# A hybrid decoder trunk: attention's TensorE work in source order, with a new pace for the work that fills it

## The chip, the core and the metric

The kernel runs on one core of a Trainium2 chip. The core has TensorE (PE; its weight loads are listed apart as PEld), VectorE (DVE), ScalarE (ACT), GpSimd (POOL) and SyncE (SP), which issues DMAs, 16 DMA engines, an on-chip memory SBUF, and a small accumulator memory PSUM of eight banks. The metric is the device time of one execution in microseconds, as the median of several runs.

## The reference

Two layers work on x (512 positions of 1024 features). With c giving shift, scale and gate vectors:

```python
h = rmsnorm(x, g_attn[layer]) * (1.0 + scale1) + shift1
o = mixer_layer(h, w_in[layer], w_out[layer], ...)
x = x + gate1 * o
h = rmsnorm(x, g_mlp[layer]) * (1.0 + scale2) + shift2
u, g = split(h @ w_up[layer])
x = x + gate2 * ((silu(causal_conv(g)) * u) @ w_down[layer])
```

The mixer projects h to queries, keys and values of 16 heads of width 64 in three groups. A (4 heads) is differential attention: two softmax maps, one subtracted from the other, with rotary embedding, and a norm of each head's output. B (6 heads) is a mixture of dilated windows, with rotary embedding. C (6 heads) has no rotary embedding but a cumulative forget bias. The heads' outputs are put side by side and multiplied with w_out. All is float32 in and out.

## The kernel before

**Numbers as pairs.** To keep float32 accuracy with a faster matmul format, a value is split into a high part (rounded, made by ACT) and a low part (the rest, made by DVE). A product is then three matmuls, hi·hi, hi·lo and lo·hi. The helper `mm3` (L250) issues them, so L251, L252 and L253 carry most of TensorE's work. Activations lie transposed, features on partitions and the 512 positions on the free axis. Weights are streamed: the class `Weights` has a plan of all chunks; SP loads a chunk of 512 KB (L148), ACT makes its high part (L174), DVE its low part (L186). `pump` is called from the matmul loops and prepares the next chunk; there are two buffers for split weights and three for raw ones.

**Attention** (`layer_attn`, L366) works on eight pairs of heads in the order B0 B1 A0 C0 A1 C1 B2 C2 (`ORDER`, L24). A pair has 8 blocks, two heads of four query blocks of 128 rows (i = 0 to 3, with 128(i+1) key columns). For a block b:

- `emit_S`: the scores, two matmuls into a PSUM bank of `ps_s` (two banks). An A pair has two maps, each with a bank of its own.
- `emit_max` (DVE L641) adds the mask and takes the row maximum; `emit_exp` (ACT L654) makes the exponential and its sum; for A, `emit_norm` (DVE L667 to L669) combines the maps.
- `emit_T`: i+1 transposes on TensorE (L682); `emit_hi` (ACT L701) and `emit_lo` (DVE L706) split the result into pth and ptl, for odd i two blocks at once.
- `emit_PV`: the products with V (L728, L729), for odd i only, into the one bank of `ps_o`.
- `head_post` (L733): two steps move a head's result out of PSUM (ACT L736, DVE L741); after the pair's second head the denominators are turned (transposes, L754), multiplied in (L756), an A pair is normalised (L763 on), and the result is split into the pair o[idx] (L240, L242).

**The loop** (L806 to L843) runs over the 64 blocks and two more. Pass b emits the transposes of block b-2, the maximum and exponential of block b, the scores of block b+1, and the P·V of block b-2. In three places it calls `fill`, which gives TensorE work of another kind. For pair idx that is: the Q and the K projection of the next pair (`qk_chunk`, 8 steps of three 512-column matmuls each), and for the first six pairs half a V projection (`v_half`, 4 steps of twelve 256-column matmuls), and in the eighth pair the output projection over the first seven pairs' results (`out_part`, 7 steps, the seventh of which needs o[6]). `fill` adds a share of the pair's cost to a credit; while the credit is over 0.3 it takes a step and subtracts 0.65 (1.3 for a V step). The shares are 0.06, 0.055 and 0.055, so 0.17 a block. Each step, and each call without one, also calls `tick`, which lets every post-processing generator in `aux` emit one step more.

**Post-processing of a projection** (`qk_post`, L446): for A and B, ACT copies the bank (L456), two DMAs swap neighbouring partitions (L458, L459), and three DVE operations apply the rotary embedding (L462 to L466). Then for B `stack_gen` splits the heads (L423, L420, L434, L436); for A the split (L240, L242) is spread by twelve DMAs of 64 KB a side (L477). For C `stack_gen` reads the bank itself, and two small DMAs add the bias rows (L443). `ready` emits what is left of this before a pair's first score.

**PSUM.** The three `mm` banks serve the projections, V's two accumulators and the first three output chunks. V's two are held from an even pair's fill to the end of the next pair's.

**What sets the order.** The source only gives an order of emission. A scheduler at build time decides each engine's order from its estimate of when things are ready, with earlier-emitted work first; on the chip each engine then runs its list in that order. `tc.issue_after(ins)` binds what is emitted inside it to stand behind `ins` on the same engine.

Of the kernel before, what the change touches and what calls it, by code (L numbers as in the profile page):

```python
# [30 lines left out]
def kernel(  # L31
# [53 lines left out]
    def tick():  # L85
        for g in list(aux):
            if next(g, StopIteration) is StopIteration:
                aux.remove(g)
# [6 lines left out]
    ident = cst[:, C_ID:C_ID + 128]  # L95
# [20 lines left out]
    for l in range(DEPTH):  # L116
# [9 lines left out]
        nout = 5  # L126
# [118 lines left out]
    def pair_tiles(pool, tag, name):  # L245
        hi = pool.tile([128, SEQ], F32R, tag=tag, name=name + "h")
        lo = pool.tile([128, SEQ], F32R, tag=tag, name=name + "l")
        return hi, lo

    def mm3(ps, w, rhs, first, last, c=slice(0, SEQ)):  # L250
        T.matmul(ps[:, c], w[0], rhs[0][:, c], start=first, stop=False, skip_group_check=True)  # L251
        T.matmul(ps[:, c], w[0], rhs[1][:, c], start=False, stop=False, skip_group_check=True)  # L252
        T.matmul(ps[:, c], w[1], rhs[0][:, c], start=False, stop=last, skip_group_check=True)  # L253

    def feat_q(ps, w, act, first=True, last=True, k0=0):
        n = len(act)
# [109 lines left out]
    def layer_attn(l, ap, mods, st, rt0):  # L366
# [21 lines left out]
        def v_half(q, half):  # L388
            nb, n = (1, VZ) if q == 0 else (2, 256)
            if half == 0:  # L390
                pools = {"m": (mm, "mm"), "t": (ps_t, "pt"), "o": (ps_o, "o")}
                vps[q] = [pools[c][0].tile([128, SEQ], F32, tag=pools[c][1], name="vps")
                          for c in ("otmt" if q == 0 else "mm")]
            pss = vps[q]
            w = W.use()
            for j in range(4):
                k = 4 * half + j
                wc = w(n * j, n * j + n)
                for tb in range(4):
                    b = slice(128 * tb, 128 * tb + 128)  # L400
                    d = pss[tb // nb][:, 256 * (tb % nb):256 * (tb % nb) + n]
                    go = k == 0 and tb % nb == 0
                    en = k == KC - 1
                    T.matmul(d, h[k][0][:, b], wc[0], start=go, stop=False, skip_group_check=True)
                    T.matmul(d, h[k][0][:, b], wc[1], start=False, stop=False, skip_group_check=True)
                    T.matmul(d, h[k][1][:, b], wc[0], start=False, stop=en, skip_group_check=True)
                W.pump(j)
                yield
            if half == 1:
                if q == 0:  # L410
                    for tb in range(4):
                        V.tensor_tensor(out=z[:, tb, :], in0=pss[tb][:, 256:VZ], in1=fb[:, l, :], op=ALU.add)
                vvs[q] = ap.tile([128, 4, 4, 128], F32R, tag="vv", name="vv", bufs=2)
                aux.append(v_post(q, lambda tb: pss[tb // nb][:, 256 * (tb % nb):256 * (tb % nb) + 256]))
# [153 lines left out]
        def out_part(m):  # L568
            ops[m] = mm.tile([128, SEQ], F32, tag="mm", name="ops") if m < 3 else ps_s.tile([128, SEQ], F32, tag="s", name="ops")
            w = W.use()  # L570
            for k in range(7):
                while o[k] is None:
                    tick()
                mm3(ops[m], w(128 * k, 128 * k + 128), o[k], k == 0, False)
                W.pump(k)
                yield

        fills = []
        for idx in range(8):
            f = []  # L580
            if idx < 7:
                f += [qk_chunk(idx + 1, 0), qk_chunk(idx + 1, 1)]
            if idx < 6:
                f += [v_half(idx // 2 + 1, idx % 2)]
            if idx == 7:
                f += [out_part(m) for m in range(nout)]
            cost = (10.4 if idx < 7 else 9.08) + (5.2 if idx < 6 else 0)
            fills.append([f, cost, 0.0])

        def fill(idx, share):  # L590
# [20 lines left out]
        def emit_S(b):  # L611
            idx, kind, hh, i = blocks[b]
            q, k = qks[idx, 0], qks[idx, 1]
            n = 128 * (i + 1)
            qb = slice(128 * i, 128 * i + 128)
            if kind != "A":
                s = ps_s.tile([128, SEQ], F32, tag="s", name="s")
                T.matmul(s[:, 0:n], q[hh][:, qb], k[hh][:, 0:n], start=True, stop=False)
                if kind == "B":
                    T.matmul(s[:, 0:n], q[hh][:, qb], k[2 + hh][:, 0:n], start=False, stop=True)  # L620
                else:
                    T.matmul(s[:, 0:n], q[2 + hh][0:68, qb], k[2 + hh][0:68, 0:n], start=False, stop=True)
                S[b] = [s]
                return
            res = []
            for mp in range(2):
                s = ps_s.tile([128, SEQ], F32, tag="s", name="s")
                T.matmul(s[:, 0:n], q[2 * hh + mp][0:96, qb], k[2 * hh + mp][0:96, 0:n], start=True, stop=True)  # L628
                res.append(s)
            S[b] = res  # L630

# [41 lines left out]
        def emit_T(b):  # L673
            i = blocks[b][3]
            e = E.pop(b)
            if i == 1:
                pt = pts[b - 1][0]
            else:
                pt = ps_t.tile([128, SEQ], F32, tag="pt", name="pt")
            for j in range(i + 1):  # L680
                c = 128 * (i + j) if i < 2 else 128 * j
                T.transpose(pt[:, c:c + 128], e[:, 128 * j:128 * j + 128], ident)  # L682
            if i % 2 == 0:
                n = (384, 1024)[i // 2]
                pts["cur"] = tuple(ap.tile([128, n], F32R, tag="%s%d" % (t, i), name=t, bufs=1) for t in ("pth", "ptl"))
            pts[b] = (pt,) + pts["cur"]
# [21 lines left out]
        def emit_PV(b):  # L708
            idx, kind, hh, i = blocks[b]
            if i % 2 == 0:  # L710
                return
            half = i // 2
            _, pth, ptl = pts.pop(b)
            pts.pop(b - 1)
            if half == 0:
                po_t["cur"] = ps_o.tile([128, SEQ], F32, tag="o", name="po")
            po = po_t["cur"]
            while running("v_post"):
                tick()
            vv = vvs[idx // 2]  # L720
            hd = 2 * (idx % 2) + hh
            nj = 2 * half + 2
            for j in range(nj):
                c0 = 128 if j == nj - 1 else 0
                oc = slice(256 * half + c0, 256 * half + 256)
                a = 256 * j if half == 0 else 256 * j + c0
                pc = slice(a, a + 256 - c0)
                T.matmul(po[:, oc], vv[:, j, hd, :], pth[:, pc], start=(j == 0), stop=False, skip_group_check=True)  # L728
                T.matmul(po[:, oc], vv[:, j, hd, :], ptl[:, pc], start=False, stop=(j == nj - 1), skip_group_check=True)  # L729
            if half == 1:  # L730
                aux.append(head_post(idx, kind, hh, po))

# [69 lines left out]

        emit_S(0)
        lag = 2
        f1, f2, f3 = 0.06, 0.055, 0.055
        for b in range(nb + lag):  # L806
            idx = blocks[min(b, nb - 1)][0]
            while idx and fills[idx - 1][0]:
                fill(idx - 1, 1.0)
            p = b - lag  # L810
            if l == 0 and b == 6:
                lpt.append(mrp.tile([128, 1024], F32, tag="raw", name="lp")[:, 0:256].rearrange(
                    "p (l j d) -> p l j d", l=DEPTH, j=4))
                nc.sync.dma_start(out=lpt[0], in_=lamp)
            if l == 0 and b == 10:
                with tc.issue_after(anchor[0]), tc.issue_after(anchor[1]):
                    prep()
            if b == 3:
                aux.append(after(fz_post()))
            if p >= 0:  # L820
                emit_T(p)
            if b < nb:
                emit_max(b)
            if p >= 0:
                emit_hi(p)
            fill(idx, f1)
            if b < nb:
                emit_exp(b)
            if p >= 0:
                emit_lo(p)  # L830
            fill(idx, f2)
            if b + 1 < nb:
                ready(b + 1)
                emit_S(b + 1)
            if b < nb:
                emit_norm(b)
            fill(idx, f3)
            if p >= 0:
                emit_PV(p)
            ms, mr = 4, 1.75  # L840
            if b >= ms:
                for _ in range(int((b - ms + 1) * mr) - int((b - ms) * mr)):
                    next(modg, None)  # L843
        aux.append(modg)
        for idx in range(8):
            while fills[idx][0]:
                fill(idx, 1.0)
        while any(g.__name__ == "head_post" for g in aux):
# [332 lines left out]
```

## Time and profile before

| | |
|---|---|
| median of 3 runs | 1338.02 us (1337.93 to 1339.64) |
| profiled execution | 1334.63 us, its span 1332.9 us |
| granted TensorE clock, mean | 0.989 |
| PE, PEld busy | 1277.8 us, 1058.6 us |
| DVE, ACT busy | 858.2 us, 642.3 us |
| attention loop, layer 0 and layer 1 | about 60 to 285 us, 700 to 922 us |

A row of the timeline has start, length, engine, line, operation, what it writes and reads, and how many were merged; in brackets stands how long the engine was idle before it and what ended that. A row by windows has the stretch, its length, the busy time of each engine with its number of instructions, the share of the TensorE clock that was granted, the busy share of the DMA engines and their rate. Matmuls are pipelined and their ends are modelled: the distance between two starts says more than the length of one.

### The profile page before, as it was taken

To read this page: it belongs to the slowest core of one execution; us is meant where nothing else is said; L and a number is where in the kernel's file an instruction comes from. 1 tells how busy PE (TensorE), PEld (TensorE's weight loads), DVE (VectorE), ACT (ScalarE), POOL (GpSimd) and SP (SyncE) were. 2 spreads that over 40 slices of the span, in tenths; PEclk is the share of its full clock that TensorE was granted. 3 is DMA by queue.
4 is the path that set the end of the run, shared out by engine and by line. 5 is a ranking of instruction groups with operands and counts; after the bars stand their busy time and mean duration, and the time that the engine had idled before them with its cause. 6 is when DMAs were issued, how large, how long until landed. Compare 5 with 4: busy or idle time off the path is not lost.

```text
span 1332.9 us, 17722 instructions
## 1 busy us (share of the span) xinstructions
PE 1277.8 (96%) x6568; PEld 1058.6 (79%) x6568; DVE 858.2 (64%) x1600; ACT 642.3 (48%) x1158; POOL 22.9 (2%) x16
## 2 busy tenths in 40 slices
PE   4899999999999999999999999999999999999997
PEld 1788888788877778888898888878878888888886
DVE  6888999868888874423347788875754444443232
ACT  5576677745333243322336677785543333333231
POOL 5100000000000000000000000000000000000000
PEclk8899999999999999999999999999999999999999
DMA  9345454433888853332432334212133333332331
GB/s 373 140 141 183 152 180 136 130 110 129 269 261 266 267 173 95 91 103 87 117 110 95 90 103 141 66 56 90 48 109 96 97 95 95 95 91 87 103 99 63
DMA packets 56601, 174.39 MB, mean 131 GB/s; under 512 B 8130, under 2 KB 10450, under 8 KB 56516
## 3 DMA queue, kind: packets, MB, share of 16 engines
q1 hardware_dynamic: 55364, 172.16, 41.0%
q8 instruction: 52, 0.85, 0.3%
q10 hardware_dynamic: 1088, 1.05, 0.2%
q14 instruction: 33, 0.27, 0.1%
q0 software_dynamic: 64, 0.06, 0.0%
HBM read 159.41 MB, written 2.10 MB: 121 GB/s over the span
## 4 chain that ended last, share of the span: by engine, by line
PE 53%; DMA 8%; DVE 7%; ACT 4%; issue 3%; SPq 0%; DVEq 0%; ACTq 0%
DMA rawm<-in_wmod_dram 7%; PE dps L251 6%; PE dps L253 6%; PE dps L252 6%; PE pu L251 4%; PE pu L253 4%; PE pu L252 4%; PE pg L252 4%; PE pg L253 4%; PE pg L251 4%; DVE wlo L186 1%; DVE rawm L217 1%; PE qkps L251 1%; PE qkps L252 1%; PE qkps L253 1%
## 5 line engine op out<-in xcount | busy, mean ns | idle before, releaser
L186 DVE TENSOR_TENSOR wlo<-raww,whi 128x1024 fp32r<-128x1024 f32 (+3 forms) x188 | 224.2, 1193 | 241.0 <-ACT whi L174 236.5
L174 ACT ACTIVATE whi<-raww 128x1024 fp32r<-128x1024 f32 (+3 forms) x188 | 194.5, 1035 | 329.6 <-PE dps L252 137.7
L253 PE MATMUL pu<-hh,wlo 128*128 128x512 f32 (+1 forms) x368 | 141.2, 384 | 3.5 <-DVE wlo L186 3.5
L252 PE MATMUL pg<-hl,whi 128*128 128x512 f32 (+1 forms) x368 | 143.0, 389 | 1.5 <-DVE hl L300 1.5
L251 PE MATMUL pg<-hh,whi 128*128 128x512 f32 (+1 forms) x368 | 141.6, 385 | 1.6 <-ACT whi L174 1.6
L251 PE MATMUL pu<-hh,whi 128*128 128x512 f32 (+1 forms) x368 | 142.4, 387 | 0.5 <-ACT whi L174 0.5
L253 PE MATMUL pg<-hh,wlo 128*128 128x512 f32 (+1 forms) x368 | 140.9, 383 | 1.1 <-DVE wlo L186 1.1
L252 PE MATMUL pu<-hl,whi 128*128 128x512 f32 (+1 forms) x368 | 140.7, 382 | 0.0
L251 PE MATMUL dps<-mh,whi 128*128 128x512 f32 x308 | 121.5, 395 | 0.0
L253 PE MATMUL dps<-mh,wlo 128*128 128x512 f32 x308 | 121.5, 394 | 0.0
L252 PE MATMUL dps<-ml,whi 128*128 128x512 f32 x308 | 121.2, 393 | 0.0
L217 DVE CUSTOM_DVE_ANT_0 rawm<-rawm,scb,bm 128x1024 f32<-128x1024 f32 x80 | 102.3, 1279 | 23.7 <-DMA rawm<-in_wmod_dram 23.4
L654 ACT ACTIVATE e<-e,nm 128x256 f32<-128x256 f32 (+3 forms) x160 | 89.0, 557 | 33.0 <-DVE nm L641 29.9
L251 PE MATMUL qkps<-hh,whi 128*128 128x512 f32 x224 | 95.1, 424 | 4.7 <-ACT qk L434 4.1
L898 ACT ACTIVATE y<-y 128x512 f32<-128x512 f32 x44 | 27.8, 632 | 142.6 <-DVE y L895 142.6
L252 PE MATMUL qkps<-hl,whi 128*128 128x512 f32 x224 | 89.7, 400 | 0.0
L253 PE MATMUL qkps<-hh,wlo 128*128 128x512 f32 x224 | 89.6, 400 | 0.0
L253 PEld LDWEIGHTS pu<-hh,wlo 128*128 128x128 f32 x368 | 69.1, 188 | 22.1 <-DVE wlo L186 6.9
L641 DVE CUSTOM_DVE_ANT_0 e<-s,cst 128x256 f32<-128x256 f32 (+3 forms) x160 | 76.4, 481 | 12.0 <-PE s L628 3.7
L252 PEld LDWEIGHTS pg<-hl,whi 128*128 128x128 f32 x368 | 69.0, 188 | 17.7 <-DVE hl L300 3.1
L253 PEld LDWEIGHTS pg<-hh,wlo 128*128 128x128 f32 x368 | 69.0, 188 | 16.7 <-DVE wlo L186 1.9
L251 PEld LDWEIGHTS pg<-hh,whi 128*128 128x128 f32 x368 | 69.1, 188 | 16.0 <-ACT whi L174 2.0
(176 smaller groups left out, 2663.2 us busy)
## 6 DMA issues: line engine op xcount, KB each, us to landing
raww<-in_wup_dram SPq DMA_DIRECT2D x88, 512.0 KB
rawm<-in_wmod_dram SPq DMA_DIRECT2D x80, 512.0 KB
raww<-in_wqk_dram SPq DMA_DIRECT2D x32, 512.0 KB
raww<-in_wdown_dram SPq DMA_DIRECT2D x32, 512.0 KB
mu<-in_wmod_dram SPq DMA_DIRECT2D x16, 512.0 KB
raww<-in_wout_dram SPq DMA_DIRECT2D x16, 448.0 KB
raww<-in_wv_dram SPq DMA_DIRECT2D x12, 512.0 KB
raww<-in_wdown_dram SPq DMA_DIRECT2D x16, 384.0 KB
```

What stands on the lines that cost most here:

```text
L174: A.activation(out=h[:, 0:m], in_=self.raw[i][:, c:c + m], func=AF.Copy)
L186: V.tensor_tensor(out=lo[:, 0:m], in0=raw[:, c:c + m], in1=h[:, 0:m].bitcast(F32), op=ALU.subtract)
L217: V.tensor_tensor_reduce(out=raw, in0=raw, in1=scb, scale=1.0, scalar=bm[:, l, ci:ci + 1], op0=ALU.mult, op1=ALU.add, accum_out=dst)
L251: T.matmul(ps[:, c], w[0], rhs[0][:, c], start=first, stop=False, skip_group_check=True)
L252: T.matmul(ps[:, c], w[0], rhs[1][:, c], start=False, stop=False, skip_group_check=True)
L253: T.matmul(ps[:, c], w[1], rhs[0][:, c], start=False, stop=last, skip_group_check=True)
L641: anchor[0] = V.tensor_tensor_reduce(out=e[:, 0:n], in0=s[:, 0:n], in1=cst[:, mask + SEQ - n:mask + SEQ], scale=-scale, scalar=3e38, op0=A ...
L654: anchor[1] = A.activation(out=e[:, 0:n], in_=e[:, 0:n], func=AF.Exp, bias=nm, scale=-1.0, accum_out=den).ins
L898: last_silu[0] = A.activation(out=y, in_=y, func=AF.Silu).ins
```

## The change

Five things change, all in `mm3` and `layer_attn`.

1. TensorE's matmuls and transposes in the loop are issued through a helper that binds each to stand behind the one before it, while `row[0]` is set (during the block loop). The matmuls in `head_post` and `fz_post` are not.
2. P·V of a block is emitted a pass later, at the end of pass b for block b-3; the loop has one pass more.
3. The fill shares depend on the block within the pair. They sum to 1 over the eight blocks, where they summed to 1.36; the first four blocks get 0.61, or 0.68 when the next pair is an A pair. The costs change accordingly.
4. Six of the seven steps of the first output chunk move from the eighth pair to the seventh. In the eighth come six steps of the second chunk, then the seventh step of the first, the seventh of the second, and the third chunk. Chunks four and five come after the loop.
5. Each pass begins with four more ticks.

```diff
+    row = [False, None]
+
+    def pe(ins):
+        with (tc.issue_after(row[1]) if row[0] and row[1] else ExitStack()):
+            r = ins()
+        row[1] = r.ins
+
+    def mmul(*a, **k):
+        pe(lambda: T.matmul(*a, **k))
+
     def mm3(ps, w, rhs, first, last, c=slice(0, SEQ)):
-        T.matmul(ps[:, c], w[0], rhs[0][:, c], start=first, stop=False, skip_group_check=True)
...
+        mmul(ps[:, c], w[0], rhs[0][:, c], start=first, stop=False, skip_group_check=True)
...
+        def part(g, n):
+            for _ in range(n):
+                next(g)
+                yield
+
+        outs = [out_part(m) for m in range(nout)]
+        near = [0.155, 0.155, 0.15, 0.15, 0.12, 0.1, 0.085, 0.085]
+        far = [0.18, 0.18, 0.17, 0.15, 0.09, 0.08, 0.075, 0.075]
+        share = [far if idx < 7 and ORDER[idx + 1][0] == "A" else [0.125] * 8 if idx == 7 else near for idx in range(8)]
...
+            if idx == 6:
+                f += [part(outs[0], 6)]
             if idx == 7:
-                f += [out_part(m) for m in range(nout)]
-            cost = (10.4 if idx < 7 else 9.08) + (5.2 if idx < 6 else 0)
+                f += [part(outs[1], 6)] + outs[0:3]
+            cost = (10.4, 9.75)[idx // 7] + (5.2 if idx < 6 else 3.9 if idx == 6 else 0)
...
-        f1, f2, f3 = 0.06, 0.055, 0.055
-        for b in range(nb + lag):
+        row[0] = True
+        for b in range(nb + lag + 1):
             idx = blocks[min(b, nb - 1)][0]
+            f1 = f2 = f3 = share[idx][b % 8] / 3 if b < nb else 0.0
+            for _ in range(4):
+                tick()
...
-            if p >= 0:
-                emit_PV(p)
+            if p >= 1:
+                emit_PV(p - 1)
...
+        row[0] = False
         aux.append(modg)
         for idx in range(8):
+            if idx == 7:
+                fills[idx][0] += outs[3:]
             while fills[idx][0]:
```

The other matmuls of the loop (V, scores, P·V) and the transposes are wrapped in the same way.

More of the change, by code (lines that the diff above doesn't have):

```diff
@@ L248, in pair_tiles @@
         return hi, lo
+    row = [False, None]
[5 more added lines that the diff above has]
+        pe(lambda: T.matmul(*a, **k))
     def mm3(ps, w, rhs, first, last, c=slice(0, SEQ)):
-        T.matmul(ps[:, c], w[0], rhs[0][:, c], start=first, stop=False, skip_group_check=True)
-        T.matmul(ps[:, c], w[0], rhs[1][:, c], start=False, stop=False, skip_group_check=True)
-        T.matmul(ps[:, c], w[1], rhs[0][:, c], start=False, stop=last, skip_group_check=True)
+        mmul(ps[:, c], w[0], rhs[0][:, c], start=first, stop=False, skip_group_check=True)
+        mmul(ps[:, c], w[0], rhs[1][:, c], start=False, stop=False, skip_group_check=True)
+        mmul(ps[:, c], w[1], rhs[0][:, c], start=False, stop=last, skip_group_check=True)
     def feat_q(ps, w, act, first=True, last=True, k0=0):
@@ L403, in v_half @@
                     en = k == KC - 1
-                    T.matmul(d, h[k][0][:, b], wc[0], start=go, stop=False, skip_group_check=True)
-                    T.matmul(d, h[k][0][:, b], wc[1], start=False, stop=False, skip_group_check=True)
-                    T.matmul(d, h[k][1][:, b], wc[0], start=False, stop=en, skip_group_check=True)
+                    mmul(d, h[k][0][:, b], wc[0], start=go, stop=False, skip_group_check=True)
+                    mmul(d, h[k][0][:, b], wc[1], start=False, stop=False, skip_group_check=True)
+                    mmul(d, h[k][1][:, b], wc[0], start=False, stop=en, skip_group_check=True)
                 W.pump(j)
@@ L617, in emit_S @@
                 s = ps_s.tile([128, SEQ], F32, tag="s", name="s")
-                T.matmul(s[:, 0:n], q[hh][:, qb], k[hh][:, 0:n], start=True, stop=False)
+                mmul(s[:, 0:n], q[hh][:, qb], k[hh][:, 0:n], start=True, stop=False)
                 if kind == "B":
-                    T.matmul(s[:, 0:n], q[hh][:, qb], k[2 + hh][:, 0:n], start=False, stop=True)
+                    mmul(s[:, 0:n], q[hh][:, qb], k[2 + hh][:, 0:n], start=False, stop=True)
                 else:
-                    T.matmul(s[:, 0:n], q[2 + hh][0:68, qb], k[2 + hh][0:68, 0:n], start=False, stop=True)
+                    mmul(s[:, 0:n], q[2 + hh][0:68, qb], k[2 + hh][0:68, 0:n], start=False, stop=True)
                 S[b] = [s]
@@ L627, in emit_S @@
                 s = ps_s.tile([128, SEQ], F32, tag="s", name="s")
-                T.matmul(s[:, 0:n], q[2 * hh + mp][0:96, qb], k[2 * hh + mp][0:96, 0:n], start=True, stop=True)
+                mmul(s[:, 0:n], q[2 * hh + mp][0:96, qb], k[2 * hh + mp][0:96, 0:n], start=True, stop=True)
                 res.append(s)
@@ L681, in emit_T @@
                 c = 128 * (i + j) if i < 2 else 128 * j
-                T.transpose(pt[:, c:c + 128], e[:, 128 * j:128 * j + 128], ident)
+                pe(lambda: T.transpose(pt[:, c:c + 128], e[:, 128 * j:128 * j + 128], ident))
             if i % 2 == 0:
@@ L727, in emit_PV @@
                 pc = slice(a, a + 256 - c0)
-                T.matmul(po[:, oc], vv[:, j, hd, :], pth[:, pc], start=(j == 0), stop=False, skip_group_check=True)
-                T.matmul(po[:, oc], vv[:, j, hd, :], ptl[:, pc], start=False, stop=(j == nj - 1), skip_group_check=True)
+                mmul(po[:, oc], vv[:, j, hd, :], pth[:, pc], start=(j == 0), stop=False, skip_group_check=True)
+                mmul(po[:, oc], vv[:, j, hd, :], ptl[:, pc], start=False, stop=(j == nj - 1), skip_group_check=True)
             if half == 1:
@@ L819, in layer_attn @@
                 aux.append(after(fz_post()))
-            if p >= 0:
+            if 0 <= p < nb:
                 emit_T(p)
@@ L823, in layer_attn @@
                 emit_max(b)
-            if p >= 0:
+            if 0 <= p < nb:
                 emit_hi(p)
@@ L828, in layer_attn @@
                 emit_exp(b)
-            if p >= 0:
+            if 0 <= p < nb:
                 emit_lo(p)
@@ L837, in layer_attn @@
             fill(idx, f3)
-            if p >= 0:
-                emit_PV(p)
+            if p >= 1:
+                emit_PV(p - 1)
             ms, mr = 4, 1.75
```

## The prediction, made before the changed kernel was run

> **What bounds the kernel now.** I read the page first, then busy time by stage, then the timeline of one engine at a time around the places where TensorE stands still.
>
> ```profile
> span 1332.9 us, 17722 instructions
> PE 1277.8 (96%) x6568; PEld 1058.6 (79%) x6568; DVE 858.2 (64%) x1600; ACT 642.3 (48%) x1158; POOL 22.9 (2%) x16
> ```
>
> TensorE bounds the whole, but 96% hides where it is loose, because pipelined matmuls are drawn longer than their spacing. The stages, two attention loops and a stretch of MLP; the columns are stretch, length, busy time of PE, PEld, DVE, ACT, POOL, clock, DMA share and rate:
>
> ```profile
> 60.00:285.00 225.00, 217.19 (x1299) 184.53 (x1298) 199.85 (x482) 161.28 (x355) 0.00 (x0) 0.99 0.50 157
> 700.00:922.00 222.00, 217.62 (x1339) 185.53 (x1338) 174.58 (x434) 159.79 (x356) 0.00 (x0) 1.00 0.30 90
> 980.00:1280.00 300.00, 300.00 (x1299) 243.65 (x1299) 126.80 (x146) 103.86 (x131) 0.00 (x0) 1.00 0.32 95
> 114.00:222.00 108.00, 103.14 (x619) 87.67 (x618) 102.27 (x257) 78.74 (x180) 0.00 (x0) 0.98 0.55 169
> 142.10:146.10 4.00, 3.96 (x14) 3.40 (x15) 3.43 (x11) 1.20 (x3) 0.00 (x0) 0.57 0.69 217
> ```
>
> The MLP stretch has 1299 matmuls in 300 us and no hole: 0.231 us each, nothing to win. The change touches only the two attention loops, 447 us together. There VectorE is the second engine: 102.3 of 108 us busy in the middle of layer 0.
>
> What a matmul really costs is the distance between starts:
>
> ```profile
> 244.01 0.39 PE L252 MATMUL qkps<-hl,whi 128*128 128x512 f32 x1
> 244.24 0.39 PE L253 MATMUL qkps<-hh,wlo 128*128 128x512 f32 x1
> 138.34 0.28 PE L404 MATMUL vps<-whi,hh 128*128 128x256 f32 x1
> 138.46 0.28 PE L405 MATMUL vps<-wlo,hh 128*128 128x256 f32 x1
> 259.26 0.66 PE L754 MATMUL pr<-cst,dx 128*128 128x128 f32 x4
> 259.67 0.31 PE L622 MATMUL s<-qk 68*128 68x128 f32 x1
> ```
>
> So 0.23 us for 512 columns, 0.12 for 256 (0.45 ns a column), and 0.41 for four transposes, 0.10 each. A head pair, from the loops of the code: 48 projection matmuls 11.0, 48 V matmuls 5.8, scores over 5120 columns 2.3, 20 transposes 2.05, P·V (16 of 256 columns, 8 of 128) 2.4, the pair's four denominator transposes 0.41. Sum 24.0 us; 18.2 for the seventh pair, which has no V. How long the pairs took is read from the first score matmul of the first and of the eighth pair, in layer 0 and in layer 1:
>
> ```profile
> 64.62 0.22 PE L618 MATMUL s<-qk 128*128 128x128 f32 x1
> 250.79 0.45 PE L618 MATMUL s<-qk 128*128 128x128 f32 x2
> 716.22 0.33 PE L618 MATMUL s<-qk 128*128 128x128 f32 x1
> 894.82 0.33 PE L618 MATMUL s<-qk 128*128 128x128 f32 x1 [0.27 <-ACT qk L434]
> ```
>
> Seven pairs took 186.2 and 178.6 us, for 6 x 24.0 + 18.2 = 162.2 of work: 24.0 and 16.4 lost, 40.4 together. That is what an order can win at most in this stretch. I estimate 8 of it as common to both kernels: the forget gate's small matmuls, the subnorm ones, and work pulled across the ends.
>
> **Where the time goes between pairs.** The next pair's scores need its K projection, which is post-processed on ACT, VectorE and SP. For the third pair (an A pair), from its last projection matmul to its first score:
>
> ```profile
> 105.74 0.40 PE L253 MATMUL qkps<-hh,wlo 128*128 128x512 f32 x1
> 108.32 0.59 ACT L456 ACTIVATE qf<-qkps 128x512 f32<-128x512 f32 x1
> 112.03 0.69 DVE L462 TENSOR_TENSOR qf<-qf,rope 128x512 f32<-128x512 f32 x1 [0.24 <-DMA sw<-qf]
> 115.41 0.62 ACT L240 ACTIVATE sw<-qf 128x512 fp32r<-128x512 f32 x1
> 116.06 0.69 DVE L242 TENSOR_TENSOR qf<-qf,sw 128x512 fp32r<-128x512 f32 x1 [0.78 <-ACT sw L240]
> 117.35 1.85 SPq L477 DMA_DIRECT2D qk<-sw  x3
> 122.89 0.29 PE L628 MATMUL s<-qk 96*128 96x128 f32 x1
> ```
>
> From 105.97 (the end of the last projection) to 122.89 is 16.9 us. TensorE did not stand still: the scheduler had pulled the pair after next's Q projection ahead of this score. The same chain in layer 1, and that of a B pair at its longest and shortest:
>
> ```profile
> 754.97 0.39 PE L253 MATMUL qkps<-hh,wlo 128*128 128x512 f32 x1
> 769.45 0.23 PE L628 MATMUL s<-qk 96*128 96x128 f32 x1
> 76.77 0.40 PE L253 MATMUL qkps<-hh,wlo 128*128 128x512 f32 x1
> 90.93 0.22 PE L618 MATMUL s<-qk 128*128 128x128 f32 x1
> 216.47 0.39 PE L253 MATMUL qkps<-hh,wlo 128*128 128x512 f32 x1
> 227.44 0.33 PE L618 MATMUL s<-qk 128*128 128x128 f32 x1
> ```
>
> 14.3 for A; 13.9 and 10.7 for B.
>
> **The change, part by part.** No matmul, transpose, load or copy is added or removed. What moves:
>
> *Order (row, pe, mmul).* Inside the loop each wrapped TensorE instruction must follow the one before it in the source, so the pulling ahead ends. If data is late, everything behind waits. The transposes of head_post and the forget gate's matmuls are not wrapped and still float.
>
> *Pace (share) and four more ticks a block.* I followed the fill rule by hand: a step is taken while the credit is over 0.3 and costs 0.65 (1.3 for V). The credit was 0.17 of the pair's cost a block, is now 0.155, 0.155, 0.15, 0.15 (0.18, 0.18, 0.17, 0.15 ahead of an A pair). The sixteen projection steps still end at the edge of the fourth and fifth block, but V's four steps spread over blocks four to seven, counted from zero, instead of ending in the fifth. From a pair's first score to the end of its last projection lie then 11.0 of projection, 1.1 of transposes, 1.2 of scores, 1.2 of P·V and 0.4 of denominators: 14.9 us (15.2 where the last step falls a block later). Behind it V and the rest make 9 us of cover, and then comes the next pair's first score, in fixed order. A pair lasts the larger of 24.0 and 14.9 plus the chain.
>
> How long the chain will be the trace does not say; bounds. Upper: as measured. Lower for A, adding the rows' own steps without queueing: copy 0.6; copy start to the first product 112.03 - 108.32 - 0.59 = 3.1 for the swap through DMA; three products of 0.69, 2.1; split 0.6 and 0.7; and 117.35 to 122.89, 5.5, for the transfers of the split halves: 12.6. For B, without those transfers and with four half-tile steps of about 0.65 (as the split rows): 8.4, so 15.2 + 8.4 lies under 24.0. I take the low ends: seven ticks a block instead of three issue a pair's Q post-processing and its SP transfers up to two blocks sooner (they ended only just ahead of K's on SP), and VectorE, whose queue stretched the rest, gets its turn whenever TensorE waits. C pairs have no swap, and I give them no loss. Four A boundaries (two a layer): 14.9 + 12.6 - 24.0 = 3.5 each, 14.0.
>
> *The bank wait.* This stop goes, as the first projection of the pair may no longer be pulled ahead of the bank's last reader:
>
> ```profile
> 139.73 0.30 PE L682 MATMUL pt<-cst,e 128*128 128x128 f32 x1
> 142.14 0.66 PE L251 MATMUL qkps<-hh,whi 128*128 128x512 f32 x1 [2.11 <-ACT qk L434]
> ```
>
> It is part of the 40.4 above and not counted again.
>
> *Q to K in odd pairs.* There V's two accumulators hold two of the three mm banks, so K's first matmul needs Q's bank copied out first. In the new pace Q's last and K's first step fall into one fill call, with nothing between. Now:
>
> ```profile
> 97.41 0.39 PE L253 MATMUL qkps<-hh,wlo 128*128 128x512 f32 x1
> 97.61 1.06 ACT L174 ACTIVATE whi<-raww 128x1024 fp32r<-128x1024 f32 x1 [1.08 <-PE qkps L252]
> 98.58 0.58 ACT L456 ACTIVATE qf<-qkps 128x512 f32<-128x512 f32 x1
> 99.21 0.50 PE L251 MATMUL qkps<-hh,whi 128*128 128x512 f32 x1
> ```
>
> 1.57 us from 97.64 to 99.21, mostly covered by P·V. Bare it costs 0.6 (the copy) to 1.57 (a weight split ahead of it). I take 0.75, nearer the copy: emitted first. Six times: 4.5.
>
> *V products a block later.* A late lo of the last transposed block no longer holds TensorE; its gain is part of the 40.4. I leave 2 us of waits of this kind.
>
> *Output projection from the seventh pair on.* Six of its steps cover the seventh pair's empty blocks (in the 40.4 again). wout's loads are issued in the same sequence, only earlier; SP carries them ahead of nothing that waits, POOL has none. But by the fill rule the seventh step, which needs the seventh pair's output, falls one block after that pair's last P·V. The chain now:
>
> ```profile
> 257.61 0.28 PE L729 MATMUL po<-ptl,vv 128*128 128x128 f32 x1
> 261.36 0.50 PE L251 MATMUL ops<-oh,whi 128*128 128x512 f32 x1 [0.23 <-ACT oh L240]
> ```
>
> 3.75 us, and in fixed order only two transposes (0.2) and the denominators (0.4) fill it: 3.1, of which 0.3 is paid now. The third output chunk's weights wait for the first's buffer: another 0.5. Two layers: 6.6. It could be nothing, if floating transposes and spare ticks bring the output sooner.
>
> A stop has a second price: after the 2.11 us above the granted clock was 0.57 for 4 us (the row 142.10:146.10), 1.7 us lost. The Trainium skill (TensorE: Matmul & The Clock Gate, "The HAM clock gate") says a whole idle window of about 3.4 us halves the clock. The 0.57 came after a shorter stop, so the trace shows less idling suffices; by the rule the 3.1 us waits would escape, by the row two of them would lose 3.4 us more, an estimate outside the sum.
>
> **Sum.** New losses in the pairs: common 8.0 + A boundaries 14.0 + Q to K 4.5 + rest 2.0 = 28.5 against 40.4: 11.9 gained. Outside: 6.6 lost. Net -5.3. The profiled execution took 1334.63 us (its span 1332.9), 3.4 under the median of 1338.02; it would come to 1329.3, and the median to **1332.7**. A measurement of this kernel tells about 0.2%, 2.7 us.
>
> **The rivals.** *Slower: the chain stays as long as measured, and TensorE may not go around it.* Place: the first score of every A and B pair. A: (16.9 + 14.3)/2 = 15.6, so 14.9 + 15.6 - 24.0 = 6.5, four times 26.0; B: (13.9 + 10.7)/2 = 12.3, so 15.2 + 12.3 - 24.0 = 3.5, four times 14.0. That is 26.0 above the low ends: 1359. It decides from a chain 0.7 us (5.3 over eight boundaries) above the low ends; B has 0.4 us of slack more. For it: VectorE at 95% in layer 0. Against: ticks and layer 1's idler VectorE. 0.32.
>
> *VectorE sets layer 0's pace.* In 114 to 222 it had 5.7 us to spare, so layer 0 gains little however TensorE is ordered: half of the 11.9 goes, 1338.7, no change. With the cases in between: 0.16.
>
> *More is won:* no wait for the output, no bare copies, chains shorter than the rows: 5.3 + 6.6 + 4.5, 1322 or better. 0.14.
>
> *The order changes nothing, because the scheduler already kept it:* the trace speaks against that; a projection started at 142.14 ahead of waiting work of the pair before. 0.02, within no change. My forecast: 0.36.
>
> **Numbers.** Faster 0.36 + 0.14 = 0.50, same 0.18, slower 0.32. The range takes in the better case with some of its A boundaries gone (1316) and most of the slower one (1355); the forecast's own is 1326 to 1337.
>
> **What would show it.** Right: score matmuls of A pairs waiting 2 to 5 us for SP's transfers, twice a layer; a 3 us wait of the output projection for oh in the eighth pair; short waits for qf; the L434 bank stop gone; seven pairs in about 180 and 173 us; an MLP stretch unchanged. Wrong: projections still ahead of scores; boundary waits of 6 us, or none; lost time elsewhere than at these places.

## The result: 7% slower

The changed kernel took 1428.98 us (median, 1425.79 to 1431.32), the kernel before 1338.53 in the same comparison: ratio 1.0677, 95% interval 1.0660 to 1.0695. The forecast had another sign, and 1428.98 lies outside its range. First the page of the profile after, and three stretches by windows (both loops and MLP; the columns are those of the prediction):

```profile
span 1427.0 us, 17757 instructions
PE 1298.2 (91%) x6568; PEld 1081.0 (76%) x6568; DVE 868.3 (61%) x1600; ACT 641.8 (45%) x1158; POOL 22.9 (2%) x16
```

```profile
60.00:330.00 270.00, 223.99 (x1287) 193.02 (x1286) 202.75 (x480) 159.60 (x353) 0.00 (x0) 0.92 0.42 129
760.00:1010.00 250.00, 209.56 (x1202) 180.12 (x1203) 166.74 (x411) 151.32 (x341) 0.00 (x0) 0.92 0.25 74
1080.00:1400.00 320.00, 320.00 (x1386) 259.81 (x1385) 133.98 (x155) 110.51 (x142) 0.00 (x0) 1.00 0.31 94
```

MLP is what it was (320 us for 1386 matmuls, 0.231 each). The windows of the loops hold somewhat fewer matmuls in more time than those of the prediction, with PE busy 83 and 84% and a granted clock of 0.92 where it was 0.99 and 1.00. The first scores of the first and eighth pair, layer 0 and layer 1:

```profile
64.48 0.27 PE L258 MATMUL s<-qk 128*128 128x128 f32 x1
297.43 0.34 PE L258 MATMUL s<-qk 128*128 128x128 f32 x2
762.95 0.33 PE L258 MATMUL s<-qk 128*128 128x128 f32 x1 [3.37 <-ACT qk L444]
985.95 0.34 PE L258 MATMUL s<-qk 128*128 128x128 f32 x2
```

Seven pairs took 233.0 and 223.0 us, where it was 186.2 and 178.6: 91.2 us more, of the 94.1 between the two profiled spans. What TensorE stood waiting for, as us in total, number of times and longest (the rows of the loops from 2.9 us on):

```profile
PE s L258 <- DMA qk<-qf: 38.1, 8, 9.5
PE pf L547 <- DVE z L539: 9.4, 2, 5.4
PE qkps L258 <- ACT qf L466: 8.4, 6, 1.4
PE pr L775 <- ACT dx L770: 8.1, 9, 1.6
PE s L258 <- ACT qk L446: 5.8, 4, 2.3
PE s L258 <- ACT qk L444: 4.2, 2, 3.4
PE sbps L784 <- ACT osq L781: 4.0, 3, 1.5
PE s L258 <- DVE nm L662: 3.4, 4, 1.4
PE ops L258 <- ACT oh L240: 2.9, 2, 1.4
```

The first row is the four first scores of the A pairs (each of two maps). The second pair's end shows how it comes about. TensorE, ACT and DVE first, then SP's queue (L468 is K's swap, L487 are the transfers of the split halves; those from 119.82 on are Q's):

```profile
120.51 0.39 PE L258 MATMUL qkps<-hh,wlo 128*128 128x512 f32 x1
122.57 0.59 ACT L466 ACTIVATE qf<-qkps 128x512 f32<-128x512 f32 x1
129.76 0.28 PE L258 MATMUL vps<-whi,hl 128*128 128x256 f32 x1
133.26 0.68 DVE L472 TENSOR_TENSOR qf<-qf,rope 128x512 f32<-128x512 f32 x1
139.49 0.47 PE L258 MATMUL s<-qk 96*128 96x128 f32 x1 [9.46 <-DMA qk<-qf]
142.75 0.45 PE L258 MATMUL s<-qk 96*128 96x128 f32 x1 [2.79 <-DMA qk<-qf]
```

```profile
119.82 1.24 SPq L487 DMA_DIRECT2D qk<-sw  x2
...
126.80 0.59 SPq L487 DMA_DIRECT2D qk<-sw  x1
127.48 0.54 SPq L468 DMA_DIRECT2D sw<-qf  x1
...
136.17 1.20 SPq L487 DMA_DIRECT2D qk<-sw  x2
```

K's last projection ends at 120.74. Its copy is done at 123.16, but SP is issuing Q's twelve transfers, about 0.6 us each, until 127.4; only then comes K's swap. From projection to score are 18.7 us, and the work written into the order ends at 130: TensorE stands 9.46 us, then 2.79 for the second map.

### The profile page after: what moved, and what is told of

It reads as the page before. It is cut to its first block, busy times and chain, and to the rows that moved or that the text cites. A ratio compares the mean times of both kernels' runs of the same rounds, so it can differ in the third digit from the quotient of the medians.

```text
span 1427.0 us, 17757 instructions
## 1 busy us (share of the span) xinstructions
PE 1298.2 (91%) x6568; PEld 1081.0 (76%) x6568; DVE 868.3 (61%) x1600; ACT 641.8 (45%) x1158; POOL 22.9 (2%) x16
## 4 chain that ended last, share of the span: by engine, by line
PE 52%; DMA 7%; DVE 7%; ACT 4%; issue 3%; SPq 0%; DVEq 0%; ACTq 0%
PE dps L258 16%; PE pu L258 12%; PE pg L258 12%; DMA rawm<-in_wmod_dram 6%; PE qkps L258 4%; PE ops L258 3%; PE vps L258 2%; DVE wlo L186 2%; DVE rawm L217 1%; PE s L258 1%; ACT whi L174 1%; PE pt L703 1%; ACT e L675 1%; PE po L258 1%; DMA raww<-in_wvz_dram 1%
## 5 line engine op out<-in xcount | busy, mean ns | idle before, releaser
L258 PE MATMUL s<-qk 128*128 128x128 f32 (+11 forms) x256 | 68.1, 338 | 51.9 <-DMA qk<-qf 38.1
L258 PE MATMUL qkps<-hh,whi 128*128 128x512 f32 x224 | 98.8, 441 | 8.4 <-ACT qf L466 8.4
L258 PEld LDWEIGHTS s<-qk 128*128 128x128 f32 (+2 forms) x256 | 47.6, 198 | 63.1 <-issue 19.4
L258 PE MATMUL qkps<-hh,wlo 128*128 128x512 f32 x224 | 90.7, 405 | 0.0
```

What stands on the lines that cost most here:

```text
L258: pe(lambda: T.matmul(*a, **k))
```

## Experiments

Each run's ratio is against the kernel before, run beside it (1335.8 to 1337.0 us in the five comparisons). "After" is the changed kernel.

**Order alone.** Pace, ticks, P·V and the output projection as before.

```diff
-            f1 = f2 = f3 = share[idx][b % 8] / 3 if b < nb else 0.0
-            for _ in range(4):
-                tick()
+            f1, f2, f3 = 0.06, 0.055, 0.055
...
-            if p >= 1:
-                emit_PV(p - 1)
+            if p >= 0:
+                emit_PV(p)
```

> The kernel before with nothing but the fixed TensorE order: old pace (0.17 a block), three ticks a block, P.V in the pass of its transposes, output projection in the eighth pair. Theory 1 (in a fixed order TensorE must stand at each pair's first score until that pair's Q and K are post-processed, and standing halves its clock): the stops at the first scores stay (48 us in the changed kernel), stops at P.V and in V's empty blocks come on top, 1410 to 1470 us. Theory 2 (the new pace, the extra ticks and the moved pieces disturb ACT, VectorE and SP, and the order itself is harmless): 1335 to 1360 us.

1424.41 us, ratio 1.0658 (1.0611 to 1.0705). The order by itself costs nearly all that the change costs, as the first theory said. Here P·V, still in its old place, held TensorE too; in the kernel after, P·V has one row of waits, 1.3 us for DVE's step out of its bank, and with the old ticks or the old pace in that order it is 0.7 and 0.6 us.

```profile
PE po L258 <- DVE ptl L725: 8.8, 12, 1.3
PE po L258 <- ACT pth L720: 5.5, 2, 3.0
```

**No order, all the rest.**

```diff
-        row[0] = True
```

> The changed kernel with only the fixed order taken out again; pace, ticks, later P.V and moved output projection stay. Theory 1: the loss goes nearly all, 1325 to 1350 us. Theory 2: most of it stays, 1390 us or more.

1359.66, ratio 1.0167 (1.0132 to 1.0202), between the two expectations. The rest is not free either; that it adds so little to the order means that it also gives something back there, P·V's waits among it.

**No order, no extra ticks.**

```diff
-        row[0] = True
...
-            for _ in range(4):
-                tick()
```

> The changed kernel without the fixed order and without the four extra ticks a block: new pace, later P.V and moved output projection are left, and the scheduler orders TensorE as before. With the order free and the ticks in, the time was 1359.7, 24 us above the kernel before. If the ticks make those 24 us (they issue post-processing in bunches), it comes to 1330-1342. If pace or later P.V make them, it stays at 1352-1364.

1341.12, ratio 1.0031 (1.0021 to 1.0042): the ticks make 18 of the 22 us.

**Only later P·V and the moved output projection.** The edit above and the old pace:

```diff
+            if idx < 7:
+                f1, f2, f3 = 0.06, 0.055, 0.055
```

> The changed kernel without the fixed order, without the extra ticks and with the old pace in the first seven pairs: later P.V and the moved output projection are all that is left. With the new pace in, the time was 1341.1, 4.5 us above the kernel before. If the new pace is what is left of the loss there, this gives 1328-1337; if the later P.V is, 1340-1346; if the new pace won something under a free order, 1346-1360.

1336.23, ratio 0.9994 (0.9980 to 1.0009): these two parts are worth nothing measurable, and the new pace costs 0.4% where the order is free.

**Projections out of the order.** The matmuls of `feat_q` and `v_half` go out as `T.matmul`, unbound; the attention's own stay bound. One line of several:

```diff
-                    mmul(d, h[k][0][:, b], wc[0], start=go, stop=False, skip_group_check=True)
+                    T.matmul(d, h[k][0][:, b], wc[0], start=go, stop=False, skip_group_check=True)
...
```

> The changed kernel, with the projection matmuls (Q, K and V of the pairs to come) out of the fixed list: they are tied to nothing and nothing is tied to them; scores, transposes, P.V and the output projection stay in their written order among themselves. Extra ticks and pace stay. Theory of the lost cover (what the scheduler used to move into the stops were projection matmuls): most of what the order costs beyond the free version's 1359.7 goes, 1355-1380. Rival (the order among the attention's own matmuls holds the score back, and floating projections can't help since the scheduler sees another time than the chip): 1400-1430.

1378.55, ratio 1.0321 (1.0286 to 1.0356). 50 us of the order's price is the binding of the projections, as the theory of the lost cover says; binding the attention's own matmuls makes the other 19. The cover can be seen: 11.1 us of projections run without a break up to the first A pair's first score, where the kernel after stood 9.46 us.

```profile
118.15 0.39 PE L261 MATMUL qkps<-hh,whi 128*128 128x512 f32 x1
...
129.00 0.40 PE L263 MATMUL qkps<-hh,wlo 128*128 128x512 f32 x1
129.47 0.22 PE L258 MATMUL s<-qk 96*128 96x128 f32 x1
```

Its waits have no row for scores waiting for DMA at all, while the bank stop at a head split, gone in after, is back:

```profile
PE s L258 <- DVE nm L662: 10.8, 12, 1.7
...
PE qkps L261 <- ACT qk L444: 4.4, 2, 2.3
```

**Order without the extra ticks.**

```diff
-            for _ in range(4):
-                tick()
```

> The changed kernel without the four extra ticks a block. Theory 1: the stops at the first scores stay or grow (post-processing is issued later), the two stops at the forget gate's matmuls (9.4 us) go: 1410 to 1450 us. Theory 2, if the ticks are what disturbs: under 1380 us.

1391.26, ratio 1.0410 (1.0365 to 1.0455): both theories missed; in the fixed order the ticks cost 38 us. Two rows of its waits against after's 38.1 and 9.4:

```profile
PE s L258 <- DMA qk<-qf: 9.6, 6, 3.5
PE pf L547 <- DVE z L539: 2.6, 2, 1.7
```

On SP K's swap now goes out behind Q's first three transfers:

```profile
116.21 0.51 SPq L487 DMA_DIRECT2D qk<-qf  x1
116.89 0.51 SPq L468 DMA_DIRECT2D sw<-qf  x1
```

From K's last projection to an A pair's first score it is 12.6, 12.8, 13.2 and 12.6 us here, and yet 54 us stay.

**Q's transfers on GpSimd's queue,** in four kernels: after, after without the order, after without the ticks, and before.

```diff
-                        nc.sync.dma_start(out=res[m][32 * j:32 * j + 32, :].bitcast(F32), in_=t[r, :].bitcast(F32))
+                        (G if side == 0 else nc.sync).dma_start(out=res[m][32 * j:32 * j + 32, :].bitcast(F32), in_=t[r, :].bitcast(F32))
```

> The changed kernel, with the twelve transfers that stack the Q side of an A pair issued by GpSimd instead of SyncE. Theory of the queue (the extra ticks put Q's twelve transfers on SP's queue ahead of K's two swap transfers, 127.48 instead of about 122.6 in the second boundary, and the score's stop of 9.5 us follows from that): K's swap goes out about 5 us sooner at the four A boundaries, the waits s<-DMA qk<-qf fall from 38.1 us to about 20, and with the clock that goes with it the time falls by 20 to 30 us, to 1399-1409. Theory of the order alone (the score has its place in the list and the chain behind K's copy is long in any case, VectorE and ScalarE being busy with other steps): K-end to score stays at 18 to 21 us and the time within 6 us of 1429.

> The changed kernel without the fixed order, ticks kept (1359.7), with Q's twelve transfers issued by GpSimd. The ticks cost 18.6 us there, and the A pairs' K-end to score is 18.9 to 22.7 us with them against 15.8 to 16.8 without. If the ticks cost by putting Q's transfers ahead of K's swap on SP, most of that comes back: 1342-1349. If they cost in another way (bunched steps on VectorE and ScalarE), 1354-1362.

> The changed kernel without the extra ticks (fixed order kept, 1391.3), with Q's twelve transfers issued by GpSimd. With the ticks the same edit gained 16 us. If SP's queue is blocked only because of the ticks, nothing is left to gain: 1387-1395. If the serial issue of the twelve transfers holds K's swap in any case, 8 to 16 us: 1375-1383.

> The kernel before, with the twelve transfers that stack the Q side of an A pair issued by GpSimd instead of SyncE; nothing of the change. There K's swap transfers stood behind only two of Q's twelve in the second boundary (about 1.2 us). If SP's queue is a price in any case, about 2 to 4 us at each of four A boundaries come back: 1322-1331. If it costs only together with the extra ticks, no difference: 1333-1340. If GpSimd issues later than SP or its transfers take longer, so that Q's stacks become the last to land: above 1340.

| kernel | plain, us | Q on GpSimd, us | ratio to before |
|---|---|---|---|
| after | 1428.98 | 1412.58 | 1.0560 (1.0544 to 1.0575) |
| after, no order | 1359.66 | 1346.53 | 1.0083 (1.0054 to 1.0111) |
| after, no ticks | 1391.26 | 1394.40 | 1.0439 (1.0409 to 1.0468) |
| before | 1336.69 | 1336.16 | 0.9998 (0.9985 to 1.0012) |

The edit gains 16 and 13 us with the extra ticks and nothing without them. So SP's queue costs through the ticks: they issue Q's transfers in one block, ahead of K's swap. In the free order the row of K's first swap, with Q on SP and with Q on GpSimd:

```profile
118.70 0.54 SPq L468 DMA_DIRECT2D sw<-qf  x1
```

```profile
112.42 0.47 SPq L468 DMA_DIRECT2D sw<-qf  x1
```

6.3 us sooner, 1.7 of them because the pair itself began sooner (its first score at 93.74 instead of 95.46). In the fixed order it is less than half of the ticks' 38 us, and 16 is under the 20 to 30 expected. The four chains fall to 16.4, 13.5, 16.0 and 13.3 us, two of them still well above those without the ticks: at the second pair's end K's swap goes out at 120.83, but the first split transfer only at 131.06, 10.2 us later, where it was 8.7 in the kernel after.

**The forget gates' matmuls.** With seven ticks a block they come to TensorE before their operand (after, first layer):

```profile
83.86 0.27 PE L258 MATMUL po<-ptl,vv 128*128 128x128 f32 x1
89.53 0.56 PE L547 MATMUL pf<-z,cst 128*128 128x6 f32 x2 [5.40 <-DVE z L539]
```

```diff
-            for _ in range(4):
+            for _ in range(12):
                 yield
             pf = ps_t.tile([128, SEQ], F32, tag="pt", name="pf")
```

> The changed kernel with eight more empty steps (12 instead of 4) between the forget gates' last vector operation and their matmuls in the first pair of each layer. With seven ticks a block the sixteen small matmuls come to TensorE 5.40 and 4.01 us before their operand is there, then run at half clock (84.1 to 93.8 us in the first layer, 9.7 us against 4.2 without the ticks). If that is a price of its own, 10 to 16 us come back: 1413-1419. If the score behind them would have waited anyway for the K chain, which runs on ScalarE and VectorE meanwhile, 0 to 5: 1424-1430.

1423.77, ratio 1.0650 (1.0613 to 1.0687), the second theory by its number. But the edit hardly did what it should, since these matmuls are unbound and the scheduler placed them early again (their stops fell only from 9.4 to 6.8 us, both layers together):

```profile
89.77 0.36 PE L547 MATMUL pf<-z,cst 128*128 128x6 f32 x2 [4.10 <-DVE z L539]
```

What this stop costs in full stays open.

**First score unbound.** The matmuls of a pair's first score block go out unbound.

```diff
+            mm_ = T.matmul if hh == 0 and i == 0 else mmul
...
-                mmul(s[:, 0:n], q[2 * hh + mp][0:96, qb], k[2 * hh + mp][0:96, 0:n], start=True, stop=True)
+                mm_(s[:, 0:n], q[2 * hh + mp][0:96, qb], k[2 * hh + mp][0:96, 0:n], start=True, stop=True)
```

> The changed kernel, except that the two matmuls of each pair's first score block are not bound into the order, so that the next pair's projections may go ahead of them. Theory 1: most of the 48 us of stops at first scores goes, and some of the half clock that follows them: 1350 to 1385 us. Theory 2: within 10 us of the changed kernel's 1429 us.

1416.84, ratio 1.0601 (1.0554 to 1.0649), a miss of both theories. Scores still waited 26.8 us for the transfers: ahead of the first A pair's score stood three projection steps (127.19 to 129.35) and then 7.00 us of stop. To free the score alone brings little cover; why the scheduler put no more there isn't shown.

**Cover written into the order.** Eight projection steps (24 matmuls, 5.5 us at 0.231 each) ahead of a pair's first score, with and without the extra ticks. The shares of the second to seventh pair are cut to 0.67 of theirs as well, so that a pair's work stays the same.

```diff
-            f1 = f2 = f3 = share[idx][b % 8] / 3 if b < nb else 0.0
+            f1 = f2 = f3 = share[idx][b % 8] / 3 * (0.67 if 0 < idx < 7 else 1.0) if b < nb else 0.0
...
+                if b % 8 == 7 and idx < 6:
+                    while fills[idx][0]:
+                        fill(idx, 1.0)
+                    fill(idx + 1, 0.33)
```

> The changed kernel with eight projection steps (24 matmuls, about 5.2 us) of the pair after next written ahead of a pair's first score, in the first six boundaries of each layer, and the shares of pairs two to seven cut to 0.67 of theirs so that the work of a pair stays the same. Theory of the lost cover (before, the scheduler itself had put projection matmuls into this place, as 115.05 to 122.03 in the second boundary; the fixed order forbids it): each of the 12 boundaries loses up to 5 us of stop, 35 to 50 us in all with what the clock gives back, 1379-1394. Rival (the post-processing, not the place of the score, sets when the next pair starts; the pulled steps only delay K's own matmuls in the pair after): stops move into the blocks, 1415-1435.

> The changed kernel without the four extra ticks a block, and with eight projection steps written ahead of a pair's first score at six boundaries a layer (shares of the other pairs cut to 0.67). Alone, the first gave 1391.3 and the second 1404.4 against 1429.0, so -37.7 and -24.6 us. If they act on separate stops (the ticks on SP's queue and on the forget gates' matmuls, the pulled steps as cover), they add: 1362-1372. If both act on the same stop, that of an A pair's first score, the second finds little left: 1384-1395.

1404.42, ratio 1.0497 (1.0481 to 1.0513), and 1382.93, ratio 1.0351 (1.0324 to 1.0379). The first lies between the theories: the boundary's stop falls from 38.1 to 8.6 us, and a third of that gain comes back inside the blocks, where scores wait 13.3 us instead of 3.4 for the bank to be read (rows of the first kernel):

```profile
PE s L258 <- DVE nm L662: 13.3, 9, 3.2
...
PE s L258 <- DMA qk<-qf: 8.6, 6, 1.8
```

Without the ticks the pulled steps gain 8 us instead of 25, about what was expected if both act on the same stop.

**The old pace in the fixed order.**

```diff
+            if idx < 7:
+                f1, f2, f3 = 0.06, 0.055, 0.055
```

> The changed kernel with the old pace of filling in the first seven pairs (0.06, 0.055, 0.055 in each block in place of the four-block shares); order, extra ticks, later P.V and moved output projection stay. If the new pace is what makes K's post-processing meet Q's (both chunks end inside four blocks, 18 to 21 us from K's end to the score at A boundaries), the old pace gives K-end to score of 13 to 15 us there, and 1400-1420. If the pace is neutral or gives K's chain the start it needs, as the prediction said, the old pace stops the score longer: 1430-1460.

1446.64, ratio 1.0823 (1.0801 to 1.0844): in the fixed order the new pace gains 18 us. The prediction had its direction right.

**The half clock.** Idle matmuls ahead of a pair's first score, in its own bank: first at all seven boundaries of a layer, then only at the A pairs and as many as fit (between the two runs the counts changed, not the way). The second edit:

```diff
+                for d in range(0 if hh or i else 6 + 2 * (idx == 2) if mp else 40 if idx == 2 else 30 - 4 * l):
+                    mmul(s, h[d % 8][0][:, 0:128], h[d % 8][0], start=True, stop=True)
                 mmul(s[:, 0:n], q[2 * hh + mp][0:96, qb], k[2 * hh + mp][0:96, 0:n], start=True, stop=True)
```

> The changed kernel with idle work on TensorE where it stands: ahead of a pair's first score 28 matmuls of 128x512 (A pairs, 6.5 us by the MLP's 0.231 us each) or 8 (the other pairs, 1.85 us) into the score's own bank, which the score then overwrites. They do nothing for the result and fill 44 us of the two layers, nearly all of it at places where TensorE stood. Theory of the half clock (the stops cost twice, since the granted clock stays low for some us behind them; 0.92 to 0.93 over the two loops, 535 us): the clock of the loops rises to 0.96 or more and the time falls by 10 to 20 us, to 1409-1419, though work was added. Rival (a stop costs its own length only, or the low clock is of no weight since ScalarE, VectorE and SP set the pace there): the time stays or grows by what of the added work isn't hidden, 1427-1445.

> The changed kernel with idle matmuls (128x512, 0.231 us, into the score's own bank, which the score overwrites) only at the A pairs' first scores, as many as fill the stops that its trace shows there: 40 and then 8 for the first A pair (9.46 and 2.79, 9.08 and 0.97 us), 30 (26 in the second layer) and then 6 for the second (7.00 and 1.40, 5.85 and 1.51). The granted clock was 0.55, 0.69, 0.73 and 0.63 in the 8 us behind these four scores, with 5.2 to 7.0 us of matmuls in them: about 8.7 us if all of the missing clock is lost. If the half clock costs what it shows, the four stretches run at 0.95 or more and the time falls by 5 to 9 us, to 1420-1424. If it costs nothing, because another chain is later anyway, 1427-1432. If the filling itself is in the way (a stop shorter than the filling), above 1432.

The first took 1435.83, ratio 1.0749 (1.0724 to 1.0774): it added work where nothing stood, and left shorter stops behind which the clock was halved all the same. The second took 1418.29, ratio 1.0607 (1.0588 to 1.0625): added work made the kernel 0.7% (9 us, by the ratios) faster. After, by windows behind the first A pair's score:

```profile
139.49:147.49 8.00, 5.21 (x17) 4.30 (x18) 3.00 (x11) 1.36 (x5) 0.00 (x0) 0.55 0.44 103
147.49:155.00 7.51, 7.51 (x41) 6.36 (x40) 6.37 (x20) 5.41 (x13) 0.00 (x0) 1.00 0.22 61
```

With the stop filled, the projections behind it run at 0.23 us at once:

```profile
137.18 0.33 PE L258 MATMUL s<-qk 96*128 96x128 f32 x1 [0.35 <-DMA qk<-qf]
...
139.91 0.39 PE L258 MATMUL qkps<-hl,whi 128*128 128x512 f32 x1
140.14 0.40 PE L258 MATMUL qkps<-hh,wlo 128*128 128x512 f32 x1
```

No kernel here beats the one before; the best (later P·V and moved output projection alone, and Q's transfers on another queue) equal it within 0.2%.

**Taken together,** one part at a time from before: P·V and output 0, pace +5, ticks +18, order of the attention's matmuls +19, projections in it +50. Parts taken in another order get other prices (the order first is +88).

## Why the prediction was wrong

**Two steps failed.** The first is the chain from K's projection to the first score: "I take the low ends: seven ticks a block instead of three issue a pair's Q post-processing and its SP transfers up to two blocks sooner". They do, and this is the harm: Q's transfers then stand on SP in front of K's swap. At A boundaries the chain took 18.7, 18.9, 18.3 and 19.2 us, above both bounds (12.6, and 16.9 or 14.3). The upper bound was taken as the chain "as measured", but that was measured with another emission; ticks change what SP has ahead of it. I had named SP's queue and looked at it for gain only.

But that is the smaller part: the A boundaries make 36.3 of the 103.1 us by which the pairs missed. Without the extra ticks the chain lay at my lower bound (12.6 to 13.2 us), and the kernel still took 1391.26, with 90.7 us lost in the pairs. So the second step is the sum's own rule, "A pair lasts the larger of 24.0 and 14.9 plus the chain". It leaves nothing for TensorE's other stops, nor for the clock behind them, once projections can't move into them: I wrote that "the pulling ahead ends" and charged the lost cover at the A boundaries alone. Everything else was given 14.5 us and lost 81.3. With free projections the whole gets 50 us back. How much of the rest is stops and how much clock isn't separated; by the two windows of the loops (0.08 of 520 us) I estimate the missing clock at 42 us at most, partly time in which TensorE stood anyway.

**Term by term,** losses of the seven pairs over 24.0 us of work (18.2 for the seventh), both layers, from the first scores in the trace:

| pairs | forecast | after |
|---|---|---|
| second and fourth, ahead of an A pair | 14.0 | 50.3 |
| third and fifth, the A pairs | 0 | 29.1 |
| first | in the common 8.0 | 27.3 |
| sixth, seventh | in the rest | 24.9 |
| Q to K, P·V, spread over them | 4.5 + 2.0 | in the rows above |
| sum | 28.5 | 131.6 |

Before they lost 40.4. The A pairs' own 29.1 comes after their score. The second map's transfers make 6.7 of it (2.79, 1.40, 0.98 and 1.51 us); the rest is half clock and small stops. It isn't the ticks' doing, as these pairs lost 28.9 without them. I had set the half clock outside the sum, as two waits' worth; four places alone gave back 9 us when filled. The first pair has the forget gates' stop, which I did not see: I noted that those matmuls float and took that for harmless, though a floating instruction still gets a fixed place when the kernel is built, and the ticks moved it ahead of its operand. The denominators' transposes and the subnorm's matmuls float too and waited 8.1 and 4.0 us (the rows pr and sbps).

**The start from work.** The estimate of 14.9 us from first score to K's end was 17.4 in the second pair, 1.4 of it the wait for Q's bank, with no other stop over 0.1 us between; and 21.7 in the first A pair, with the second map's 2.79 us and the half clock behind it.

**The rivals.** The slower one, "TensorE may not go around it", has the right mechanism and was given 1359. It charged only the excess of the chain over 24.0 at the eight boundaries where it looked; that the lost cover makes 50 us is shown by the run with free projections. VectorE's limit did not come to bear: in layer 0's loop it was 75% busy after (202.75 of 270 us).

**What was right.** MLP untouched; the bank stop at a head split gone; short waits for Q's bank, six times 1.40 (8.4 in all against 4.5); P·V's waits almost gone (1.3 against 2.0 left), worth nothing in the free order and against 14.3 us in the fixed order with P·V in its old place. The output projection's wait in the eighth pair came as forecast, 3.2 us in each layer against 3.1, if all three stops of that chain are counted (1.54, 1.44 and 0.23 in layer 0):

```profile
307.70 0.66 PE L775 MATMUL pr<-cst,dx 128*128 128x128 f32 x4 [1.54 <-ACT dx L770]
309.81 0.50 PE L258 MATMUL ops<-oh,whi 128*128 128x512 f32 x1 [1.44 <-ACT oh L240]
```

The granted clock was 0.50 behind it (310.50 to 313.80, and 1000.00 to 1003.30 in layer 1), as the estimate outside the sum had it.

The sign named as wrong, "boundary waits of 6 us", is what the profile shows.

## What to carry to other kernels

A fixed order takes away the work that a scheduler moves into waits, all waits and not only the one in view: before binding an engine's instructions, look in the trace for what ran ahead of its place at every long wait, and write that work there yourself. When emission steps are made more frequent, list each queue they feed and what then stands in front of the transfer that a long chain waits for. Bounds from a chain measured under one emission do not bound it under another.

## What the runs showed of the hardware

SP issued transfers of 64 KB one after another, about 0.6 us each (the median of 64 is 588 ns), so a dozen held the next transfer over 7 us. And a stop need not be long for the clock to fall: in the first run with idle matmuls in front of the scores, the fourth pair's end had two stops of 0.66 and 1.56 us with one short score between, and the projections behind ran 0.43 us apart for 3 us:

```profile
209.43 0.30 PE L258 MATMUL s<-qk 96*128 96x128 f32 x1 [0.66 <-DMA qk<-qf]
211.29 0.30 PE L258 MATMUL s<-qk 96*128 96x128 f32 x1 [1.56 <-DMA qk<-qf]
...
212.54 0.63 PE L258 MATMUL qkps<-hh,wlo 128*128 128x512 f32 x1
212.97 0.63 PE L258 MATMUL qkps<-hh,whi 128*128 128x512 f32 x1
```

Nor does a stop's length alone decide. A single stop of 1.40 us in after left the clock alone: 103.33 to 120.74, with that stop in it, has a granted clock of 1.00. One of 1.39 us at 168.58, with 0.11 us beside it, was followed by 0.50 from 170.50 to 173.90. And of the two bank stops of the kernel before, the prediction took its price from the first, of 2.11 us (0.57 behind it); the second, of 2.04 us, ends at 198.50 and cost no clock:

```profile
198.50:202.00 3.50, 3.50 (x19) 2.88 (x20) 3.50 (x12) 1.97 (x5) 0.00 (x0) 1.00 0.67 205
```

The rule of a whole idle window of about 3.4 us (the Trainium skill, TensorE: Matmul & The Clock Gate, "The HAM clock gate") does not cover these short stops; why some sufficed and others did not is not settled.
